# Ranking the experts of a mixture-of-experts layer by token count and giving the three smallest 64 rows

## The chip, the cores and the metric

The kernel runs on one core of a Trainium2 chip. The metric is the device time of one execution in microseconds (us), the median of several runs.

## What is computed

The reference is a model of two parts on 256 tokens with 1024 channels. The first part has two layers (neighbourhood attention, an RWKV recurrence and a convolution side by side, then a feed-forward network), the second part two more layers of another kind. The feed-forward network of the first part's second layer is the mixture of experts (MoE) that the change is about:

```python
logits = (xt @ router).astype(jnp.float32)
top_logit, top_e = lax.top_k(logits, TOP_K)          # 2 of 8 experts per token
gates = jax.nn.softmax(top_logit, axis=-1)
...
def expert_block(args):
    x_blk, e = args
    return _swiglu(x_blk, w_gate[e], w_up[e], w_down[e])   # silu(x Wg) * (x Wu), then Wd
...
y = jnp.zeros_like(xt).at[s_tok].add(yb[dest] * s_gate[:, None].astype(xt.dtype))
```

An expert's weights are `w_gate` and `w_up` of 1024x3584 and `w_down` of 3584x1024, all float32. There are 512 assignments of a token to an expert in all. With the inputs used here the experts 0 to 7 get 66, 72, 53, 98, 54, 53, 64 and 52 of them; this follows from the reference's router and is the same in every run.

## The kernel before

**Arithmetic.** A float32 operand is split in two parts that TensorE (PE) can multiply: hi is the operand rounded, lo is what is left. `split` (L180) makes hi with a cast on ScalarE (ACT, L182) and lo with a subtraction on VectorE (DVE, L183). A product x·w is then three products of parts: x hi by w hi, x lo by w hi, x hi by w lo (`projT`, L267). All of them are issued at L154; transposes on PE at L158.

**Weights.** `wload` (L185) starts a 1 MB load on the SP queue into one of 5 buffers `wr`, and splits the tile in two chunks of 128x1024 into `wh` (ACT) and `wl` (DVE), of which there are 5 buffers each. A `wr` buffer comes free when its second `wl` is written; a `wh` or `wl` buffer when PE has used it.

**One expert.** The MoE runs expert after expert, 0 to 7, each with 128 slots for tokens. First the tokens of a pair of experts are gathered: `one_hot` (L1272, DVE) makes the matrix `oh` of tokens by slots from `pos`, the slot of each token, and 32 products of `oh` with the hi and lo part of the tokens put the gathered tokens, transposed, in PSUM; ACT copies the hi part to `xH` (L1205), DVE the lo part to `xL` (L1206). An expert's 3584 hidden columns are 7 blocks of 512. A block is `gate_up` (L1160): four chunks of `w_gate` and four of `w_up`, 48 products into two PSUM banks, silu on ACT (L1171) and the product of the two, `s`, on DVE (L1172); and `down` (L1175): four transposes of `s`, their split into `aH` (ACT) and `aL` (DVE), and four chunks of `w_down`, 24 products. That is 6 loads, 12 casts, 12 subtractions and 72 products of 512 columns. `down` of a block stands behind `gate_up` of the next. At the expert's end `y` is scaled and split (L1244 on ACT, L1245 on DVE), `back` (L1262) multiplies it with the transposed one-hot matrix `ohT`, and DVE adds the result to `moe_out` (L1251). While expert 7 ends, the second part's first weights are loaded and the residual is added (L1037).

**Routing.** Ahead of the gather DVE compares the logits, makes `sel` (which token has which expert), and PE counts: `pp` holds each token's slot and, in its third row, each expert's count. `pos` (L1130) is the slot, or over 4096 where a token doesn't use the expert. The largest count goes to a register (`most`, L1210); where it is over 128 an extra pass (`overflow`, L1294) runs ahead of expert 2. With these inputs it does not.

**Order.** The instructions of the MoE stand on each engine's queue in an order that a scheduler chose at build time; each engine works through its queue in order.

## Time and profile before

| | us |
|---|---|
| median of 3 runs (2878.35 to 2884.21) | 2883.58 |
| the profiled execution, its own time | 2886.99 |
| its span, first to last instruction | 2885.2 |
| MoE, first gather's first product to the last `w_down` product | 1240.96 to 2283.88 |
| experts 5, 6 and 7, from expert 4's `y` to expert 7's | 1900.28 to 2284.32 |

The span is followed with a profile of one execution: how long each engine (PE with its weight loads PEld, DVE, ACT, POOL and the DMA engines) was busy, which waits ended last (the chain), and single instructions in order of time. Starts are us from the start of the span. "Granted clock" is the share of full speed that TensorE was given in a stretch: 1.00 is 2.4 GHz, 0.5 would be 1.2 GHz.

### The profile page before, as it was taken

To read this page: it belongs to the slowest core of one execution; us is meant where nothing else is said; L and a number is where in the kernel's file an instruction comes from. 1 tells how busy PE (TensorE), PEld (TensorE's weight loads), DVE (VectorE), ACT (ScalarE), POOL (GpSimd) and SP (SyncE) were. 2 spreads that over 40 slices of the span, in tenths; PEclk is the share of its full clock that TensorE was granted. 3 is DMA by queue.
4 is the path that set the end of the run, shared out by engine and by line. 5 is a ranking of instruction groups with operands and counts; after the bars stand their busy time and mean duration, and the time that the engine had idled before them with its cause. 6 is when DMAs were issued, how large, how long until landed. Compare 5 with 4: busy or idle time off the path is not lost. (4 is left out here: it accounts for less than half of the span.)

```text
span 2885.2 us, 42860 instructions
## 1 busy us (share of the span) xinstructions
PE 2750.6 (95%) x17006; PEld 2257.8 (78%) x17006; DVE 1988.4 (69%) x2753; ACT 1468.3 (51%) x2032; POOL 348.5 (12%) x256
## 2 busy tenths in 40 slices
PE   6998999999998879999989999999999999999999
PEld 4677656778886766677867777778777889998999
DVE  4685474322225796488878888888889868856784
ACT  3313243322224332477757777767777646644563
POOL 1420012211001610100000000000000221301120
PEclk9898799999999998999999999999999999999999
DMA  6122155333333224579988999899989835553453
GB/s 227 51 74 74 52 150 193 96 123 94 97 99 105 81 88 140 173 293 352 319 321 325 322 353 344 328 338 362 337 325 349 307 114 175 183 183 117 161 184 109
DMA packets 108098, 585.77 MB, mean 203 GB/s; under 512 B 12657, under 2 KB 19825, under 8 KB 54129
## 3 DMA queue, kind: packets, MB, share of 16 engines
q1 hardware_dynamic: 107888, 582.95, 57.5%
q8 instruction: 136, 2.23, 0.3%
q14 instruction: 74, 0.60, 0.1%
HBM read 580.80 MB, written 2.10 MB: 202 GB/s over the span
## 5 line engine op out<-in xcount | busy, mean ns | idle before, releaser
L183 DVE TENSOR_TENSOR wl<-wr,wh 128x1024 fp32r<-128x1024 f32 x978 | 1169.5, 1225 | 477.9 <-ACT wh L182 465.6
L182 ACT CAST wh<-wr 128x1024 fp32r<-128x1024 f32 x992 | 1003.8, 1044 | 681.1 <-PE psffn L154 193.2
L154 PE MATMUL psmoe<-wh,xH 128*128 128x512 f32 x896 | 354.9, 397 | 3.4 <-ACT wh L182 3.4
L154 PE MATMUL psmoe<-wl,xH 128*128 128x512 f32 x896 | 356.2, 398 | 1.0 <-DVE wl L183 0.7
L154 PE MATMUL psmoe<-wh,xL 128*128 128x512 f32 x896 | 355.5, 397 | 0.0
L154 PEld LDWEIGHTS psmoe<-wl,xH 128*128 128x128 f32 x896 | 168.3, 188 | 45.6 <-DVE wl L183 6.5
L154 PEld LDWEIGHTS psmoe<-wh,xH 128*128 128x128 f32 x896 | 168.4, 188 | 44.4 <-ACT wh L182 5.0
L154 PE MATMUL pssf<-oh,wl 128*128 128x256 f32 x704 | 199.5, 284 | 0.0
L154 PE MATMUL pssf<-ohT,wh 128*128 128x256 f32 x704 | 199.2, 284 | 0.0
L154 PEld LDWEIGHTS psmoe<-wh,xL 128*128 128x128 f32 x896 | 168.4, 188 | 39.1
L154 PE MATMUL pssf<-oh,wh 128*128 128x256 f32 x704 | 198.9, 284 | 0.0
L154 PE MATMUL psmoe<-wh,aL 128*128 128x512 f32 x448 | 178.3, 398 | 2.0 <-DVE aL L183 2.0
L154 PE MATMUL psmoe<-wh,aH 128*128 128x512 f32 x448 | 175.6, 397 | 2.5 <-ACT aH L182 2.5
L154 PE MATMUL psmoe<-wl,aH 128*128 128x512 f32 x448 | 163.3, 400 | 0.0
L1551 POOL TENSOR_SCALAR x<-x,fin 128x256 f32<-128x256 f32 x8 | 12.2, 1542 | 1057.5 <-DMA wr<-w_in 1057.3
L154 PE MATMUL psffn<-h2L,wh 128*128 128x512 f32 x352 | 138.7, 394 | 1.3 <-POOL h2L L257 1.3
L154 PE MATMUL psffn<-h2H,wh 128*128 128x512 f32 x352 | 138.2, 395 | 1.0 <-ACT h2H L256 1.0
L154 PE MATMUL psffn<-h2H,wl 128*128 128x512 f32 x352 | 137.5, 392 | 0.0
L154 PEld LDWEIGHTS pssf<-oh,wl 128*128 128x128 f32 x704 | 135.2, 192 | 0.0
L154 PEld LDWEIGHTS pssf<-ohT,wh 128*128 128x128 f32 x704 | 135.1, 192 | 0.0
L154 PEld LDWEIGHTS pssf<-oh,wh 128*128 128x128 f32 x704 | 135.0, 192 | 0.0
L154 PEld LDWEIGHTS psmoe<-wh,aL 128*128 128x128 f32 x448 | 84.2, 188 | 24.4 <-DVE aL L183 4.4
(476 smaller groups left out, 5624.6 us busy)
## 6 DMA issues: line engine op xcount, KB each, us to landing
wr<-moe_w_gate SPq DMA_DIRECT2D x112, 1024.0 KB, 7.0
wr<-moe_w_up SPq DMA_DIRECT2D x112, 1024.0 KB, 6.6
wr<-moe_w_down SPq DMA_DIRECT2D x112, 1024.0 KB, 7.0
wm<-mod_w SPq DMA_DIRECT2D x96, 512.0 KB, 4.3
wr<-f_up SPq DMA_DIRECT2D x44, 1024.0 KB, 4.9
wr<-w_in SPq DMA_DIRECT2D x52, 512.0 KB, 3.8
wr<-w_in SPq DMA_DIRECT2D x16, 1024.0 KB, 5.0
wr<-f_down SPq DMA_DIRECT2D x16, 1024.0 KB, 5.0
```

Of the source, the lines that this page charges most:

```text
L154: i = self.nc.tensor.matmul(out, lhsT, rhs, start=start, stop=stop, **kw)
L182: self.nc.scalar.copy(H, src)
L183: (eng or self.nc.vector).tensor_sub(L, src, H.bitcast(F32))
L1551: nc.gpsimd.tensor_scalar(x[:, k], x[:, k], fin[:, k:k + 1], None, op0=ALU.mult)
```

## The change

**Ranking.** Between the counting and `pos`, DVE ranks the experts by count, largest first, with ties in order of number; expert 0 gets the key 1024, so it keeps place 0. `pm` is the 8x8 permutation. `pos`, the counts and the gate weights `wt` are permuted into the order of places (`placed`). `who` holds the expert of each place.

**Weights by register.** SP reads seven places of `who` into registers at expert 1; the loads of places 1 to 7 take the address of the weights from the register (`at`).

**Places 5 to 7** have 64 slots. The hi and lo parts of their tokens stand side by side in one stationary operand of 64 + 64 columns, so that one product with w hi and one with w lo give x hi·w in the rows 0 to 63 of PSUM and x lo·w in the rows 64 to 127: a load takes 8 products in place of 12, a block 48 in place of 72. For gate and up the two halves are added ("fold"): ACT copies the rows 64 to 127 to SBUF, DVE adds the rows 0 to 63. Silu works on 64 rows, the product `s` is made on POOL, the transposes are 64 columns wide, and `aH` and `aL` become the halves of one tile. The halves of `w_down`'s result are not folded: `ohT` of these places has the 64 one-hot rows twice, so `back` adds them.

**Gathers.** Places 0 and 1, and 2 and 3, are gathered as before; place 4 alone, 5 and 6 together with 64 products of 64 columns, and 7 alone with 32. `overflow` starts at 64 rows for the small places.

```diff
-                nc.vector.tensor_tensor(pos, pp[:, 0:2], off, ALU.add)
+                cnt = pr.tile([128, 8], F32, name="cnt")
+                key = pr.tile([128, 8], F32, name="key")
+                nc.vector.tensor_copy(cnt, pp[:, 2])
+                nc.vector.tensor_copy(key, cnt)
+                nc.vector.memset(key[:, 0:1], 1024.0)
+                i8 = self.iota[:, 0:8]
+                sq8, lt2 = [128, 8, 8], lt[:, 0]
+                a, c = key[:, None, :].to_broadcast(sq8), key[:, :, None].to_broadcast(sq8)
+                kg, ke = gt[:, 0], eq[:, 0]
+                nc.vector.tensor_tensor(kg, a, c, ALU.is_gt)
+                nc.vector.tensor_tensor(ke, a, c, ALU.is_equal)
+                nc.vector.tensor_tensor(ke, ke, lt2, ALU.mult)
+                nc.vector.tensor_add(kg, kg, ke)
+                rank = pr.tile([128, 8], F32, name="rank")
+                nc.vector.tensor_reduce(rank[:, :, None], kg, AX.X, ALU.add)
+                nc.vector.tensor_tensor(pm, rank[:, None, :].to_broadcast(sq8), i8[:, :, None].to_broadcast(sq8), ALU.is_equal)
+                def placed(o, v):
+                    for tt in range(2):
+                        w = pr.tile(sq8, F32, tag="plw", name=self.nm("plw"), bufs=2)
+                        nc.vector.tensor_tensor(w, pm, v[:, tt, None, :].to_broadcast(sq8), ALU.mult)
+                        nc.vector.tensor_reduce(o[:, tt, :, None], w, AX.X, ALU.add)
+                nc.vector.tensor_tensor(off, pp[:, 0:2], off, ALU.add)
+                placed(pos, off)
...
+                self.at = lambda n, j: A[n][0] if j == 0 else A[n][bass.ds(self.place[j], 1)][0]
...
+                                if e < SMALL:
+                                    self.projT(ps, H, L, xh, xl, [(k, k0 + k) for k in range(2)], slice(0, 128), k0 == 0, k0 == 6)
+                                    continue
+                                for k in range(2):
+                                    self.mm(ps, xh[:, k0 + k], H[:, k], k0 + k == 0, False, chain=ps)
+                                    self.mm(ps, xh[:, k0 + k], L[:, k], False, k0 + k == 7, chain=ps)
...
-                    nc.scalar.activation(s, pp[0], AF.Silu)
-                    nc.vector.tensor_mul(s, s, pp[1])
-                    return s
+                    if e < SMALL:
+                        nc.scalar.activation(s, pp[0], AF.Silu)
+                        nc.vector.tensor_mul(s, s, pp[1])
+                        return s
+                    two = []
+                    for ps in pp:
+                        t = pg.tile([64, 512], F32, tag="fold", name=self.nm("fold"))
+                        nc.scalar.copy(t, ps[64:128])
+                        nc.vector.tensor_add(t, ps[0:64], t)
+                        two.append(t)
+                    nc.scalar.activation(s[0:64], two[0], AF.Silu)
+                    nc.gpsimd.tensor_mul(s[0:64], s[0:64], two[1])
+                    return s[0:64]
...
-                    aL = pg.tile([128, 4, 128], F32R, tag="aL", name=self.nm("aL"))
-                    self.split(aH, aL, pt)
+                    aL = aH[:, :, 64:128] if n == 64 else pg.tile([128, 4, 128], F32R, tag="aL", name=self.nm("aL"))
+                    self.split(aH[:, :, 0:n], aL, pt)
...
+                                if n == 128:
+                                    self.mm(py[o], aL[:, kh * 2 + k], H[:, 0, c], False, False, chain=py[o])
...
+                def gather_small(e0, n, t):
+                    X = pg.tile([128, 8, 2, 128], F32R, tag=t, name=self.nm(t))
+                    for k in range(KT):
+                        ps = self.ps((128, n, 2, 64))
+                        for i, src in enumerate((hmH, hmL)):
+                            for j in range(n):
+                                for tt in range(2):
+                                    self.mm(ps[:, j, i], src[:, tt, k * 128:(k + 1) * 128], oh[:, tt, e0 + j, 0:64], tt == 0, tt == 1, chain=ps)
+                        (nc.vector.tensor_copy if k % 2 else nc.scalar.copy)(X[:, k, 0:n], ps.rearrange("p a b s -> p a (b s)"))
...
+                    if e == 1:
+                        self.place = [None] + [nc.values_load(who[0:1, j:j + 1], engines=(mybir.EngineType.SP,), min_val=0, max_val=7) for j in range(1, E)]
```

**How the order moves.** Line numbers of the changed kernel lie one higher at the helpers (L182 becomes L183, L183 becomes L184) and further on up to a hundred higher. The first place is DVE's queue between the counting and the first one-hot matrix `oh`. Before (`hmL` is the lo part of the tokens, `h` the tokens scaled, `mx` and `over` the largest count):

```order
L1129 TENSOR_SCALAR off<-sel 128x16
L183 TENSOR_TENSOR hmL<-h_9945,hmH 128x512
L1130 TENSOR_TENSOR pos<-psrout_9906,off 128x16
L1146 SCALAR_TENSOR_TENSOR h_9949<-psrout_9930,rr_9875,sb 128x512
L1275 TENSOR_TENSOR oh<-cst,pos 128x2x256
L1149 TENSOR_REDUCE mx<-psrout_9906 128x1
L183 TENSOR_TENSOR hmL<-h_9949,hmH 128x512
L1150 CAST over<-mx 128x1
L183 TENSOR_TENSOR wl_10028<-wr_10021,wh_10027 128x1024
```

In the changed kernel the same stretch, in two pieces; the first begins behind `off` (`cnt`, `key`, `gt`, `eq`, `ixw` and `plw` belong to the ranking):

```order
L1136 COPY cnt<-psrout_9908 128x8
L1159 TENSOR_TENSOR off<-psrout_9908,off 128x16
L1137 COPY key<-cnt 128x8
L184 TENSOR_TENSOR hmL<-h_9965,hmH 128x512
L1138 MEMSET key 128x1
L1176 SCALAR_TENSOR_TENSOR h_9969<-psrout_9950,rr_9877,sb 128x512
L1143 TENSOR_TENSOR gt<-key 128x64
L1144 TENSOR_TENSOR eq<-key 128x64
L1183 COPY ixw<-cnt 128x8
L184 TENSOR_TENSOR wl_10061<-wr_10054,wh_10060 128x1024
L1145 TENSOR_TENSOR eq<-eq,cs_r 128x64
L184 TENSOR_TENSOR hmL<-h_9969,hmH 128x512
```

The second piece follows it and ends with `oh`:

```order
L1146 TENSOR_TENSOR gt<-gt,eq 128x64
L184 TENSOR_TENSOR wl_10079<-wr_10076,wh_10078 128x1024
L1148 TENSOR_REDUCE rank<-gt 128x8
L184 TENSOR_TENSOR wl_10083<-wr_10076,wh_10082 128x1024
L1150 TENSOR_TENSOR pm<-rank,cst 128x64
L184 TENSOR_TENSOR wl_10102<-wr_10099,wh_10101 128x1024
L1156 TENSOR_TENSOR plw_9929<-pm,off 128x64
L1156 TENSOR_TENSOR plw_9932<-pm,off 128x64
L1157 TENSOR_REDUCE pos<-plw_9929 128x8
L1157 TENSOR_REDUCE pos<-plw_9932 128x8
L1156 TENSOR_TENSOR plw_9978<-pm,ixw 128x64
L1368 TENSOR_TENSOR oh<-cst,pos 128x2x256
```

Ahead of `oh` there stand now sixteen small instructions of the ranking and placing in place of one, one `hmL` more, and four subtractions `wl` of the first weight chunks that stood behind it.

The second place is a block of a small expert in its steady state. ACT's queue before, from the silu of a block to the cast of its `aH` (`wh` are the casts of the chunks, a pair for each load):

```order
L1171 ACTIVATE s_19150<-psmoe_19060 128x512
L182 CAST wh_19130<-wr_19128 128x1024
L182 CAST wh_19134<-wr_19128 128x1024
L182 CAST wh_19164<-wr_19162 128x1024
L182 CAST wh_19168<-wr_19162 128x1024
L182 CAST wh_19186<-wr_19184 128x1024
L182 CAST wh_19190<-wr_19184 128x1024
L182 CAST aH_19304<-psmoe_19299 128x512
L182 CAST wh_19209<-wr_19207 128x1024
```

ACT's queue in the changed kernel, from the silu of a block to a cast behind its `aH_19424`:

```order
L1228 ACTIVATE s_19283<-fold_19284 64x512
L183 CAST wh_19302<-wr_19300 128x1024
L183 CAST wh_19306<-wr_19300 128x1024
L1225 COPY fold_19287<-psmoe_19246 64x512
L183 CAST wh_19320<-wr_19318 128x1024
L183 CAST wh_19324<-wr_19318 128x1024
L183 CAST aH_19424<-psmoe_19419 128x4x64
L183 CAST wh_19339<-wr_19337 128x1024
L183 CAST wh_19343<-wr_19337 128x1024
```

Six casts stood between the silu and `aH`; now four stand there and the copy for the fold of `up`, two of them behind that copy, and `aH` stands ahead of the casts of the next gate load (`wr_19337`). DVE's queue before, from the last chunk ahead of `s` to one behind the `aL` made from it:

```order
L183 TENSOR_TENSOR wl_19165<-wr_19162,wh_19164 128x1024
L1172 TENSOR_TENSOR s_19150<-s_19150,psmoe_19105 128x512
L183 TENSOR_TENSOR wl_19169<-wr_19162,wh_19168 128x1024
L183 TENSOR_TENSOR wl_19187<-wr_19184,wh_19186 128x1024
L183 TENSOR_TENSOR wl_19191<-wr_19184,wh_19190 128x1024
L183 TENSOR_TENSOR aL_19305<-psmoe_19299,aH_19304 128x512
L183 TENSOR_TENSOR wl_19210<-wr_19207,wh_19209 128x1024
```

DVE's queue in the changed kernel, over the same piece of a block as ACT's:

```order
L1226 TENSOR_TENSOR fold_19284<-psmoe_19209,fold_19284 64x512
L184 TENSOR_TENSOR wl_19268<-wr_19265,wh_19267 128x1024
L184 TENSOR_TENSOR wl_19272<-wr_19265,wh_19271 128x1024
L184 TENSOR_TENSOR wl_19303<-wr_19300,wh_19302 128x1024
L184 TENSOR_TENSOR wl_19307<-wr_19300,wh_19306 128x1024
L1226 TENSOR_TENSOR fold_19287<-psmoe_19246,fold_19287 64x512
L184 TENSOR_TENSOR wl_19321<-wr_19318,wh_19320 128x1024
L184 TENSOR_TENSOR wl_19325<-wr_19318,wh_19324 128x1024
L184 TENSOR_TENSOR aH_19424<-psmoe_19419,aH_19424 128x4x64
L184 TENSOR_TENSOR wl_19340<-wr_19337,wh_19339 128x1024
```

Two folds have taken the place of `s`, and two `wl`, where three stood, lie between the last of them and the subtraction that fills the second half of `aH`.

## Rows read from the trace of the kernel before

**Rows 1.** Windows, experts 5-7: us, busy PE PEld DVE ACT POOL, clock, DMA, GB/s.

```profile
1900.28:2284.32 384.04, 378.36 (x1689) 301.89 (x1687) 333.72 (x328) 275.10 (x308) 0.00 (x0) 1.00 0.93 344
```

**Rows 2.** Chain that ended last, part of expert 3: start us, us, what.

```profile
1705.34 16.80 PE psmoe L154 x72
1722.14 0.44 PE psmoe L158 x4
```

**Rows 3.** Groups by form, same window: count, busy us, mean ns, idle before.

```profile
L183 DVE TENSOR_TENSOR wl<-wr,wh 128x1024 fp32r<-128x1024 f32 x251 | 293.6, 1219 | 31.5 <-ACT wh L182 29.3 <-PE psmoe L154 0.8
L182 ACT CAST wh<-wr 128x1024 fp32r<-128x1024 f32 x251 | 248.2, 1050 | 18.0 <-PE psmoe L154 17.7
L182 ACT CAST aH<-psmoe 128x512 fp32r<-128x512 f32 x21 | 12.3, 587 | 31.4 <-PE psmoe L158 31.4
L1251 DVE TENSOR_TENSOR moe_out<-moe_out,psmoe 128x512 f32<-128x512 f32 x12 | 7.7, 681 | 0.1
L1245 DVE SCALAR_TENSOR_TENSOR y<-psmoe,gs,y 128x512 fp32r<-128x512 f32 x6 | 4.2, 746 | 6.9 <-ACT y L1244 6.9
L1037 DVE SCALAR_TENSOR_TENSOR x<-moe_out,modt,x 128x256 f32<-128x256 f32 x8 | 3.6, 475 | 0.0
```

**Rows 4.** DVE in time, expert 5: start us, us, instruction [idle before <-releaser].

```profile
1907.19 8.03 DVE L183 TENSOR_TENSOR wl<-wr,wh 128x1024 fp32r<-128x1024 f32 x7
1915.13 0.68 DVE L1172 TENSOR_TENSOR s<-s,psmoe 128x512 f32<-128x512 f32 x1
1915.73 4.62 DVE L183 TENSOR_TENSOR wl<-wr,wh 128x1024 fp32r<-128x1024 f32 x4
```

**Rows 5.** POOL, then DVE, in time, second part of the model.

```profile
2419.65 2.14 POOL L1597 TENSOR_TENSOR moe_out<-moe_out 128x512 f32<-128x512 f32 x1 [13.04 <-DVE moe_out L1639]
...
2449.88 1.30 POOL L1597 TENSOR_TENSOR moe_out<-moe_out 128x512 f32<-128x512 f32 x1 [6.12 <-DVE moe_out L1639]
...
2420.55 1.91 DVE L1638 SCALAR_TENSOR_TENSOR moe_out<-u,prs,moe_out 128x255 f32<-128x255 f32 x2
...
2448.87 0.87 DVE L1639 SCALAR_TENSOR_TENSOR moe_out<-u,prs,moe_out 128x255 f32<-128x255 f32 x2
```

**Rows 6.** Windows in expert 0, columns as in Rows 1.

```profile
1256.00:1266.00 10.00, 10.00 (x45) 8.04 (x44) 9.99 (x11) 9.85 (x11) 0.00 (x0) 1.00 1.01 423
1320.00:1340.00 20.00, 20.00 (x88) 16.08 (x87) 17.80 (x17) 15.31 (x16) 0.00 (x0) 1.00 1.00 380
```

**Rows 7.** DVE, then PE, in time around the first gather.

```profile
1240.13 0.68 DVE L1275 TENSOR_TENSOR oh<-cst,pos 128x512 fp32r<-128x512 f32 x1
1240.73 0.16 DVE L1149 TENSOR_REDUCE mx<-psrout 128x1 f32<-128x8 f32 x1
...
1240.96 0.77 PE L154 MATMUL psmoe<-oh,hmH 128*128 128x256 f32 x2 [1.61 <-DVE mx L1149]
...
1242.37 0.63 PE L154 MATMUL psmoe<-oh,hmL 128*128 128x256 f32 x2
1242.80 0.63 PE L154 MATMUL psmoe<-oh,hmH 128*128 128x256 f32 x2
...
1246.51 0.40 PE L154 MATMUL psmoe<-wh,xH 128*128 128x512 f32 x1
```

**Rows 8.** Instructions of line 1210 by engine: minimum, median, maximum ns.

```profile
L1210 SPq TENSOR_LOAD <-over x1: 469/469/469, 1284.0 to 1284.0; - x1
```

**Rows 9.** PE in order of time at the end of expert 7.

```profile
2283.88 0.63 PE L154 MATMUL psmoe<-wl,aH 128*128 128x512 f32 x2
...
2292.35 0.39 PE L154 MATMUL pssp<-hmH,wh 128*128 128x256 f32 x1 [0.33 <-ACT wh L182]
```

**Rows 10.** Windows where PE waits often, columns as in Rows 1.

```profile
980.00:1000.00 20.00, 14.28 (x58) 11.48 (x60) 17.37 (x24) 4.71 (x7) 16.43 (x9) 0.66 0.16 42
1236.00:1246.00 10.00, 7.32 (x38) 7.28 (x39) 8.10 (x19) 4.62 (x10) 0.00 (x0) 0.56 0.33 111
```

More of the change, by code (lines that the diff above doesn't have):

```diff
@@ L25 @@
 FE = 3584
+SMALL = 5
 FF = 2816
@@ L1167, in gate_up @@
                                 k0 = kh * 4 + i * 2
-                                self.projT(ps, H, L, xh, xl, [(k, k0 + k) for k in range(2)], slice(0, 128), k0 == 0, k0 == 6)
+                                if e < SMALL:
[4 more added lines that the diff above has]
+                                    self.mm(ps, xh[:, k0 + k], L[:, k], False, k0 + k == 7, chain=ps)
@@ L1175, in down @@
+                    nc.scalar.activation(s[0:64], two[0], AF.Silu)
+                    nc.gpsimd.tensor_mul(s[0:64], s[0:64], two[1])
+                    return s[0:64]
                 def down(e, fb, s, py):
[L1176 removed]
+                    n = s.shape[0]
+                    pt = self.ps((128, 4, n))
                     for k in range(4):
[L1178 removed]
+                        self.tp(pt[:, k], s[:, k * 128:(k + 1) * 128], self.ident[0:n, 0:n], chain=pt)
@@ new lines, in moe, with gather @@
+                xs = {}
+                def gather(e0, n, tag):
+                    H, L = [pg.tile([128, 8, 2, 128], F32R, tag=t, name=self.nm(t)) for t in ("xH", "xL")]
+                    for k in range(KT):
+                        ps = self.ps((128, 2, n * 128), tag=tag)
+                        for i, src in enumerate((hmH, hmL)):
+                            for tt in range(2):
+                                self.mm(ps[:, i], src[:, tt, k * 128:(k + 1) * 128], oh[:, tt, e0:e0 + n].rearrange("p a s -> p (a s)"),
+                                        tt == 0, tt == 1, chain=ps)
+                        nc.scalar.copy(H[:, k, 0:n].rearrange("p a s -> p (a s)"), ps[:, 0])
+                        nc.vector.tensor_copy(L[:, k, 0:n].rearrange("p a s -> p (a s)"), ps[:, 1])
+                    for i in range(n):
+                        xs[e0 + i] = H[:, :, i], L[:, :, i]
@@ new lines, in gather_small @@
+                def gather_small(e0, n, t):
+                    X = pg.tile([128, 8, 2, 128], F32R, tag=t, name=self.nm(t))
+                    for k in range(KT):
+                        ps = self.ps((128, n, 2, 64))
+                        for i, src in enumerate((hmH, hmL)):
+                            for j in range(n):
+                                for tt in range(2):
+                                    self.mm(ps[:, j, i], src[:, tt, k * 128:(k + 1) * 128], oh[:, tt, e0 + j, 0:64], tt == 0, tt == 1, chain=ps)
+                        (nc.vector.tensor_copy if k % 2 else nc.scalar.copy)(X[:, k, 0:n], ps.rearrange("p a b s -> p a (b s)"))
+                    for i in range(n):
+                        xs[e0 + i] = X[:, :, i], None
@@ new lines, in moe @@
+                for e in range(E):
+                    if e == 0:
+                        gather(0, 2, "pp")
+                    elif e == 2:
+                        self.overflow(out, hmH, hmL, oh, ohT, gs, pos, wt, most, pg)
+                        self.one_hot(oh, pos, 2, 0)
+                        gather(2, 2, "ax")
+                    elif e == 4:
+                        self.one_hot(oh, pos, 4, 0, 1)
+                        for j in range(SMALL, E):
+                            self.one_hot_small(oh, pos, j)
+                        gather(4, 1, "ax")
+                    elif e == 5:
+                        gather_small(5, 2, "xH")
+                    elif e == 7:
+                        gather_small(7, 1, "xL")
+                    xh, xl = xs[e]
@@ L1228, in moe @@
                         nc.vector.reciprocal(mx, mx)
-                        nc.vector.tensor_tensor(wt, wt, mx.to_broadcast([128, 2, 8]), ALU.mult)
+                        nc.vector.tensor_tensor(lg, wt, mx.to_broadcast([128, 2, 8]), ALU.mult)
+                        for tt in range(2):
+                            w = pg.tile([128, 8, 8], F32, tag="s", name=self.nm("wtw"))
+                            nc.vector.tensor_tensor(w, pm, lg[:, tt, None, :].to_broadcast([128, 8, 8]), ALU.mult)
+                            nc.vector.tensor_reduce(wt[:, tt, :, None], w, AX.X, ALU.add)
                     if e % 2 == 0:
@@ L1298, in overflow @@
             w_ = lambda i: pg.tile([128, 8, 2, 128], F32R, tag=("xH", "xL")[i], name=self.nm("wo")).bitcast(F32).rearrange("p a b c -> p (a b c)")
+            for e in range(E):
+                self.one_hot(oh, pos, e, 128 if e < SMALL else 64, 1)
             for e in range(0, E, 2):
-                self.one_hot(oh, pos, e, 128)
                 self.slots(oh, ohT, gs, wt, e)
```

53 lines of the change are left out of this document (24 added, 29 removed).

## The prediction

> **What bounds the kernel now.** I looked first at the stretch in which the small experts will stand, experts 5 to 7 [rows 1]. The reader is to see that PE is busy for 378.36 of 384.04 us at a granted clock of 1.00, the higher of its two levels, 2.4 GHz, while DVE has 333.72, ACT 275.10, POOL nothing, and the DMA engines a share of 0.93. The chain of waits says the same: a block is 16.80 us of 72 products and 0.44 us of transposes, 17.24 us, with nothing between [rows 2]. A product is thus 16.80 / 72 = 0.233 us. So products taken away shorten the stretch, but only down to what comes next, and DVE and the DMA engines are close behind.
>
> **The change part by part.** *The block of a small expert.* PE: 48 × 0.233 + 0.44 = 11.6 us at most, 5.6 less than now. The loads stay at six of 1.0486 MB, 6.29 MB. In two windows the DMA engines were busy throughout, at 423 and at 380 GB/s [rows 6]; a block then takes 14.9 or 16.55 us. I take the lower rate, the one of the longer window. DVE: seven subtractions in a row take 8.03 us [rows 4], 1.147 each, so twelve are 13.76. An operation of 128x512 that reads PSUM keeps DVE for 0.60 (from 1915.13 to 1915.73 [rows 4]). A fold has the same 512 elements in each row, 0.61 with its start; two are 1.22. The lo half of `aH` has half of them: 0.35, an estimate from that 0.60. The product `s` goes from DVE to POOL. Together 15.33 us.
>
> Two things are added on DVE's side. POOL's product has no row of its own in this shape; the nearest is POOL's product of the same row length, 1.30 us by itself and 2.14 beside DVE [rows 5]. In that second case two DVE operations that otherwise take 0.87 took 1.91 [rows 5]: 1.04 us lost on DVE each time. The bounds are 0 (nothing overlaps) and 1.3 (DVE stands for the whole of POOL's operation); I take the measured 1.04. The second is the way from the fold of `up` to `aL`: POOL up to 2.14, four transposes 0.44, the cast of `aH` on ACT (0.59 for twice the size [rows 3]), and only then ACT's next cast `wh`, 1.05 [rows 3], for which DVE waits. From the end of the fold that is 2.14 + 0.44 + about 0.4 + 1.05 = 4.0 us, with the hand-overs some 4.35. DVE has meanwhile two subtractions, the stop and the lo half: 2.3 + 1.04 + 0.35 = 3.7. So it waits about 0.7, between 0 (POOL undisturbed at 1.30) and 1.5. Before, six casts stood there and hid it all.
>
> Sum of a block on DVE: 15.33 + 1.04 + 0.7 = 17.07 us against 17.24 on PE: almost nothing is gained. Without the two additions the DMA engines set 16.55; with both at their upper ends it is 15.33 + 1.3 + 1.5 = 18.1. ACT has twelve casts at some 0.97, two copies, a silu and `aH`, under 14 us, and is no bound.
>
> *The three experts.* 21 blocks are 21 × 17.07 = 358.5 us. To them come what DVE does at the experts' ends: 4.2 + 7.7 for `y` and `moe_out`, 3.6 for the residual [rows 3], and about 2.4 for its half of the gathers' copies, 17.9 in all. And DVE's waits while PE gathers. At the higher clock a product of 256 columns takes half of the 0.233 us, 0.12; narrower ones have no row here, and I give them the same price as their upper end, so 64 and 32 products are 7.7 and 3.8 us. At the three ends together that is 0 (DVE has five free `wl` buffers, 5.7 us, to work ahead) to 11.5; I take 6.8. Sum 358.5 + 17.9 + 6.8 = 383.2 against 384.04: **−0.8 us**.
>
> *The routing.* Here PE stands and waits for DVE: the first gather product starts at 1240.96, just when `oh` is written [rows 7], and the first product of expert 0 follows the gather at once, at 1246.51 [rows 7], so a late `oh` is paid in full. In the new order 15 more small instructions stand ahead of `oh`, an `hmL`, and four `wl`. A small one takes 0.16 [rows 7], with its start 0.17: 2.55. `hmL`, 128x512, is 0.60 as above. Four `wl` at 1.147 are 4.59. **+7.7 us**. The `wl` are not lost work, but behind `oh` they cost nothing, since PE was busy without a pause there [rows 6]. The bounds: 3.2 if the subtractions fall into waits of DVE, 9 if each small one waits for the one before it.
>
> *The registers.* Eight reads in place of one on SP, 0.469 us each [rows 8], and one more register instruction before each of 294 loads. Loads stand far enough ahead, five `wr` buffers and as many `wh` and `wl`; if that cover is gone at expert 1, the seven reads cost at most 7 × 0.47 = 3.3 us. I take 0.
>
> *The end.* From the last MoE product at 2283.88 to the second part's first weights at 2292.35 [rows 9] PE waits for little. With DVE full, fewer of those chunks are split ahead: **+1**, between 0 and 4.6 (four chunks). The gather that moves from experts 6 and 7 to smaller ones, the permuted `wt` (a few 0.17 us instructions) and the other experts' blocks, which remain at 17.24, cost nothing more, since PE sets their time.
>
> Sum: −0.8 + 7.7 + 1 = +7.9 us on the profiled execution's 2886.99. That one is 0.12% above the median of the runs shown; on the median, 2883.58 + 7.9 = **2891.5 us**.
>
> A rule of the Trainium skill speaks against the change. The rows show the core loading at 380 to 423 GB/s [rows 6]. "DMA: Bandwidth & Descriptors", section "Where 436 GB/s comes from", says that transfers from HBM to SBUF are held to about 358 GB/s for each core. By it a block's loads would take 17.57 us, the three experts about 10 us more than in my sum, and the whole about 2902. The trace goes above that figure, so the sum doesn't use it; slower loads have a place among the rivals.
>
> **The rivals.**
> *The loads or DVE's bare work are the bound (0.30).* POOL's product falls where DVE waits anyway, and ACT runs ahead far enough. For it: in this stretch DVE waited 31.5 us for casts [rows 3], time in which a stop costs nothing. Against it: with DVE the last to be ready there is less such time. A block is then between 15.6 (DVE's 15.33 and a little, loads at 423 GB/s) and the loads' 16.55. The whole is 7.9 − 21 × (17.07 − block): at 16.55 it is −3, 2880.6; at 15.6 it is −23, 2860.6; in the middle, at 16.2, −10.4, **2873**. It decides from a block below 16.4 us on: there the whole is 5.8 us faster.
>
> *The way through the fold is longer (0.14).* Behind the copy for the fold of `up` ACT's casts wait until PE has done the last product of `up`, which waits for DVE's last `wl` of it; two engines then hold each other up in turn. Against it: two `wl` stand on DVE between that chunk and the fold. At 18.1 us for a block the stage is 21 × 1.03 = 22 us longer than in my sum: 2913.
>
> *The loads are slower than in expert 0 (0.04).* If they never go above this stage's mean of 344 GB/s [rows 1], a block takes 18.3 us: 21 × 1.2 = 26 more than in my sum, 2917. Against it stand both windows [rows 6].
>
> *TensorE's clock falls (0.09).* With 11.6 of 17 us of work PE has pauses in each block. In one stretch with 14.28 of 20 us busy the granted clock was 0.66, in one with 7.32 of 10, behind a longer wait, 0.56 [rows 10], so part of it at the lower level of 1.2 GHz. There two products of 256 columns, as many columns as one of 512, started 0.43 us after the two before [rows 7]. A block is then 48 × 0.43 + 0.44 = 21.1, 4.0 over DVE's; in a quarter of the blocks that is 21 us, 2913. Against it: the pauses are about a microsecond each, spread over the block. "TensorE: Matmul & The Clock Gate", section "HAM oscillation — how this bites in real kernels", of the Trainium skill describes a kernel whose products are shorter than the wait for their next operand, so that it falls to the lower clock at each step.
>
> That the change doesn't do what it says: with 53, 53 and 52 tokens the three small places hold all of theirs, and place 1 has 98, so the extra pass stays out; the order shows 48 products a block. I give it nothing.
>
> **How the numbers follow.** A measurement of this kernel can tell about 0.2%, 5.8 us, from no change. The forecast has 0.43. Its own range is 2882 to 2903: the routing's 3.2 to 9, the register reads' 3.3, the end's 4.6 and part of the block's spread. I put 0.24 of it over 2889.3 (slower), 0.18 within and 0.01 under. The first rival gives 0.26 faster and 0.04 same (at 16.4 to 16.55), the three others 0.27 slower. Together 0.27 faster, 0.22 same, 0.51 slower. The range goes from 2864, a block of 15.8 us in the first rival, to 2914; outside lie the slower loads, half of the clock and of the longer fold, and the far end of the first rival.
>
> **What would show it.** In the profile after, a small expert's block should have DVE busy or stopped throughout, about 17.1 us long, with PE waiting for `wl` and `wh` over five microseconds a block; `oh` written near 1248.5 and the first gather there; experts 0 to 4 unchanged between their `y`; POOL's `s` at about 2 us, with a DVE operation beside it some 1 us too long. I am wrong if blocks take under 16.7 or over 17.7 us, if DVE's operations beside POOL aren't longer, or if the gather starts before 1244.

## The result and the profile after

The changed kernel takes 2918.93 us in the median of 4 runs (2914.35 to 2924.86); the kernel before takes 2882.01 (2878.35 to 2884.21, 4 runs). The ratio is 1.0131, 95% interval 1.0108 to 1.0153, so 31 to 44 us slower. I had forecast 2891.5 with a range of 2864 to 2914: slower, as forecast, but by four to five times as much, and outside the range.

The profiled execution took 2920.04 us, its span is 2918.3 against 2885.2 before. Experts 5 to 7 now run from 1889.15 to 2319.45, 430.3 us against 384.04 [rows 1]. The windows of that stretch, of ten microseconds in expert 5's gather and of one block in its steady state (columns as in rows 1):

```profile
1889.15:2319.45 430.30, 340.95 (x1248) 243.19 (x1248) 339.74 (x348) 287.38 (x349) 79.43 (x21) 0.85 0.83 306
1900.00:1910.00 10.00, 10.00 (x45) 9.71 (x45) 1.27 (x3) 1.12 (x3) 0.00 (x0) 0.50 0.01 2
2011.99:2030.14 18.15, 14.84 (x54) 9.68 (x53) 15.33 (x16) 13.43 (x17) 3.31 (x1) 0.91 0.93 367
```

PE and the loads both have less to do in a microsecond than before (PE busy for 340.95 of 430.30 us, DMA share 0.83, where it was 378.36 of 384.04 and 0.93 [rows 1]), and DVE is no busier: nothing is full. The granted clock is 0.85 over the stretch, and 0.50, the lower level of 1.2 GHz, in the gather. The groups of instructions from 2060 to 2160 say who waits (busy us, mean ns, idle before and its releaser):

```profile
L184 DVE TENSOR_TENSOR wl<-wr,wh 128x1024 fp32r<-128x1024 f32 x63 | 73.3, 1217 | 5.4 <-ACT wh L183 5.2
...
L1229 POOL TENSOR_TENSOR s<-s,fold 64x512 f32<-64x512 f32 x6 | 19.8, 3308 | 94.8 <-DVE fold L1226 94.8
...
L159 PE MATMUL psmoe<-cst,s 64*128 64x64 f32 x24 | 3.3, 271 | 16.7 <-POOL s L1229 16.7
L184 DVE TENSOR_TENSOR aH<-psmoe,aH 128x256 fp32r<-128x256 f32 x6 | 2.5, 425 | 13.0 <-ACT aH L183 13.0
...
L183 ACT CAST aH<-psmoe 128x256 fp32r<-128x256 f32 x6 | 2.2, 372 | 20.8 <-PE psmoe L159 20.8
```

POOL's `s` takes 3308 ns, where before a product of the same row length took 1.30 us by itself [rows 5]. PE's transposes wait for it (16.7 us for six blocks), ACT's cast `aH` for them, and DVE's lo half of `aH` for that cast, 13.0 us for six blocks. In order of time, two blocks of POOL:

```profile
1936.68 5.51 POOL L1229 TENSOR_TENSOR s<-s,fold 64x512 f32<-64x512 f32 x1 [10.40 <-DVE fold L1226]
...
2011.99 3.31 POOL L1229 TENSOR_TENSOR s<-s,fold 64x512 f32<-64x512 f32 x1 [14.62 <-DVE fold L1226]
```

and DVE around them:

```profile
1935.85 0.68 DVE L1226 TENSOR_TENSOR fold<-psmoe,fold 64x512 f32<-64x512 f32 x1 [1.09 <-ACT fold L1225]
1936.46 4.61 DVE L184 TENSOR_TENSOR wl<-wr,wh 128x1024 fp32r<-128x1024 f32 x4
```

```profile
2011.23 0.68 DVE L1226 TENSOR_TENSOR fold<-psmoe,fold 64x512 f32<-64x512 f32 x1
2011.84 2.34 DVE L184 TENSOR_TENSOR wl<-wr,wh 128x1024 fp32r<-128x1024 f32 x2
2016.48 0.42 DVE L184 TENSOR_TENSOR aH<-psmoe,aH 128x256 fp32r<-128x256 f32 x1 [2.30 <-ACT aH L183]
2017.42 6.90 DVE L184 TENSOR_TENSOR wl<-wr,wh 128x1024 fp32r<-128x1024 f32 x6 [0.52 <-ACT wh L183]
```

The reader is to see when POOL ends. Beside two subtractions that end at 2011.84 + 2.34 = 2014.18 its product lasts until 2015.30; beside four that end at 1941.07 it lasts until 1942.19. Both times that is about 1.1 us after DVE's last subtraction: what is left of POOL's product once DVE stands still is nearly the whole of it. In all 21 blocks it ends 1.12 us after the last of two to five such subtractions, and none of them is lengthened. ACT in the second of the two blocks:

```profile
2010.15 0.58 ACT L1225 COPY fold<-psmoe 64x512 f32<-64x512 f32 x1 [0.28 <-PE psmoe L155]
...
2016.08 0.37 ACT L183 CAST aH<-psmoe 128x256 fp32r<-128x256 f32 x1 [3.44 <-PE psmoe L159]
```

Its copy for the fold of `up` waits only 0.28 us for PE; the long wait, 3.44 us, is the one at `aH`, behind POOL's `s` and the transposes.

The other engine to look at is PE while it has all 72 products. The chain in expert 3, which the change leaves as it was:

```profile
1710.08 16.52 PE psmoe L155 x72
1726.61 0.44 PE psmoe L159 x4
```

A block of 72 products takes 16.52 us; before it was 16.80 [rows 2]. And around the first gather, the first cast of the tokens' hi part on ACT, `oh` on DVE and the first gather product on PE:

```profile
1223.98 0.62 ACT L183 CAST hmH<-h 128x512 fp32r<-128x512 f32 x1 [2.58 <-DVE h L1176]
```

```profile
1238.19 0.68 DVE L1368 TENSOR_TENSOR oh<-cst,pos 128x512 fp32r<-128x512 f32 x1
```

```profile
1239.02 0.76 PE L155 MATMUL psmoe<-oh,hmH 128*128 128x256 f32 x2 [9.10 <-DVE ix L1157]
```

The same cast before:

```profile
1233.40 0.62 ACT L182 CAST hmH<-h 128x512 fp32r<-128x512 f32 x1 [2.58 <-DVE h L1146]
```

From that cast to the first gather product it was 1240.96 − 1233.40 = 7.6 us [rows 7], and is 1239.02 − 1223.98 = 15.0. The cast itself came 9.4 us earlier; the instructions up to it are the same in both kernels but for one small copy on DVE (`ixw`), and in the profiles of the experiments it stands between 1217.7 and 1239.5, so that is the spread of executions.

The spans differ by 33.1 us, and that is made up of: −9.4 up to that cast; +7.5 to the first gather; −9.2 from there to expert 4's `y` (659.3 before, 650.1 after); +46.3 in experts 5 to 7; −2.0 behind them.

### The profile page after: what moved, and what is told of

Same layout as the page of the kernel before. It is cut to its first block, busy times and chain, and to the rows that moved or that the text cites. A ratio compares the mean times of both kernels' runs of the same rounds, so it can differ in the third digit from the quotient of the medians.

```text
span 2918.3 us, 42695 instructions
## 1 busy us (share of the span) xinstructions
PE 2696.3 (92%) x16566; PEld 2193.1 (75%) x16566; DVE 2002.1 (69%) x2802; ACT 1475.8 (51%) x2072; POOL 418.7 (14%) x277
## 4 chain that ended last, share of the span: by engine, by line
PE 37%; DVE 5%; POOL 3%; issue 3%; ACT 2%; ACTq 0%; DVEq 0%; POOLq 0%
PE psmoe L155 16%; PE pssf L155 13%; PE pssp L155 4%; DVE wl L184 3%; POOL s L1229 3%; PE psssg L155 2%; ACT wh L183 1%; PE pssat L155 1%; PE psmoe L159 1%; DVE fold L1226 1%; PE pssat L159 0%; DVE moe_out L1344 0%; ACT s L1228 0%; ACT y L1337 0%; DVE x L1038 0%
## 5 line engine op out<-in xcount | busy, mean ns | idle before, releaser
L184 DVE TENSOR_TENSOR wl<-wr,wh 128x1024 fp32r<-128x1024 f32 x978 | 1181.6, 1239 | 459.2 <-ACT wh L183 446.6
L183 ACT CAST wh<-wr 128x1024 fp32r<-128x1024 f32 x992 | 1000.5, 1044 | 645.3 <-PE psffn L155 193.2
L155 PE MATMUL psmoe<-wl,xH 128*128 128x512 f32 x784 | 321.5, 411 | 10.0 <-DVE wl L184 9.9
L155 PE MATMUL psmoe<-wh,xH 128*128 128x512 f32 x784 | 315.6, 404 | 3.6 <-ACT wh L183 3.6
L155 PE MATMUL psmoe<-wh,xL 128*128 128x512 f32 x672 | 269.4, 401 | 0.0
L1229 POOL TENSOR_TENSOR s<-s,fold 64x512 f32<-64x512 f32 x21 | 79.4, 3782 | 1010.6 <-DVE fold L1226 1010.6
L155 PEld LDWEIGHTS psmoe<-wl,xH 128*128 128x128 f32 x784 | 151.9, 194 | 65.5 <-DVE wl L184 33.1
L155 PEld LDWEIGHTS psmoe<-wh,xH 128*128 128x128 f32 x784 | 153.0, 195 | 36.8 <-ACT wh L183 6.5
L155 PEld LDWEIGHTS psmoe<-wh,xL 128*128 128x128 f32 x672 | 129.5, 193 | 27.4 <-ACT wh L183 0.2
L155 PE MATMUL psmoe<-wh,aL 128*128 128x512 f32 x280 | 110.4, 394 | 0.6 <-DVE aL L184 0.6
L155 PEld LDWEIGHTS psmoe<-wl,aH 128*128 128x128 f32 x448 | 86.7, 206 | 28.7 <-DVE wl L184 11.3
```

Source lines behind the costliest of these rows:

```text
L155: i = self.nc.tensor.matmul(out, lhsT, rhs, start=start, stop=stop, **kw)
L183: self.nc.scalar.copy(H, src)
L184: (eng or self.nc.vector).tensor_sub(L, src, H.bitcast(F32))
L1229: nc.gpsimd.tensor_mul(s[0:64], s[0:64], two[1])
```

## The experiments

Three questions came from this. What makes experts 5 to 7 longer: POOL's product that can't go on (called the port theory: POOL and DVE both read SBUF then, and one would keep the other out), or TensorE's clock? What do ranking and registers cost by themselves? And why do the unchanged products take 16.52 us? Times of before in each comparison are those of the same chip in the same hours, so kernels of different experiments are best compared by their ratios.

### 1. `s` on DVE

```diff
-                    nc.gpsimd.tensor_mul(s[0:64], s[0:64], two[1])
+                    nc.vector.tensor_mul(s[0:64], s[0:64], two[1])
```

> The changed kernel with one word altered: the product s of the small experts is made on DVE, not on POOL. Port theory: in the changed kernel POOL's product lasts 3.31 to 6.66 us because it doesn't go on while DVE works through its subtractions, and the chain fold, s, transposes, aH, next cast waits for it. On DVE it takes about 0.6 us, a block becomes 15.3 + 0.6 = 15.9 us of DVE or what the loads allow (16.6 to 17.1), the three experts take some 375 us in place of 430, and the whole about 2864. Clock theory: the granted clock of 0.85 in that stretch is what lengthens it; then it stays near 430 and the whole over 2905.

Measured: 2869.19 us in the median (10 runs), before 2879.82 (25), ratio 0.997 (0.995 to 0.999). One word turns 1.3% slower into 0.3% faster. Experts 5 to 7 take 368.7 us. The stretch and one block (columns as in rows 1), then DVE in that block:

```profile
1893.18:2261.86 368.68, 326.32 (x1248) 209.06 (x1248) 348.13 (x369) 288.24 (x349) 0.00 (x0) 0.96 0.92 355
2066.88:2082.76 15.88, 14.02 (x54) 8.43 (x53) 15.84 (x17) 13.57 (x17) 0.00 (x0) 1.00 1.01 410
```

```profile
2066.88 0.68 DVE L1229 TENSOR_TENSOR s<-s,fold 64x512 f32<-64x512 f32 x1
2067.49 2.34 DVE L184 TENSOR_TENSOR wl<-wr,wh 128x1024 fp32r<-128x1024 f32 x2
2069.76 0.41 DVE L184 TENSOR_TENSOR aH<-psmoe,aH 128x256 fp32r<-128x256 f32 x1
2070.10 6.88 DVE L184 TENSOR_TENSOR wl<-wr,wh 128x1024 fp32r<-128x1024 f32 x6
```

DVE is busy for 15.84 of 15.88 us, with no wait at `aH` or behind it, and the loads run at 410 GB/s. The wait is gone with POOL's product, as the port theory has it; the clock theory falls, as the clock came back to 1.00 by itself when the wait was gone. The runs show that POOL's product stands still beside DVE; that a port of SBUF is the reason is argued, not shown.

### 2. A wait more: DVE stands still for POOL

```diff
                     nc.gpsimd.tensor_mul(s[0:64], s[0:64], two[1])
+                    t = pg.tile([64, 8], F32, tag="mark", name=self.nm("mark"))
+                    self.mark = nc.vector.tensor_copy(t, s[0:64, 0:8]).ins.name
...
+        if self.after_mark is not None:
+            self.tc.add_manual_dep(i.ins, self.after_mark, NOSYNC, reason="behind the mark")
```

> The changed kernel with s still on POOL, and one tiny DVE copy that reads s, put ahead of the two subtractions that stand between the fold of up and aH, so that DVE stands still while POOL makes s. It only adds a wait and an instruction. Port theory: POOL's product takes about 1.2 us, DVE loses 1.3 us a block but the 2.8 us that it waited for aH and the next cast go; a block is near 16.9 us, the whole about 2874. Rival (DVE is the bound and every wait adds): 21 times 1.3 us more, about 2945.

Measured: 2888.92 us (9 runs), ratio 1.0032 (1.001 to 1.0055): 30 us less than the changed kernel by an instruction and a wait that were added. POOL, then DVE, in one block:

```profile
1993.06 1.26 POOL L1232 TENSOR_TENSOR s<-s,fold 64x512 f32<-64x512 f32 x1 [15.53 <-DVE fold L1229]
```

```profile
1992.23 0.68 DVE L1229 TENSOR_TENSOR fold<-psmoe,fold 64x512 f32<-64x512 f32 x1
1994.36 0.16 DVE L1234 COPY mark<-s 64x8 f32<-64x8 f32 x1 [1.44 <-POOL s L1232]
1994.46 2.36 DVE L185 TENSOR_TENSOR wl<-wr,wh 128x1024 fp32r<-128x1024 f32 x2
1996.74 0.42 DVE L185 TENSOR_TENSOR aH<-psmoe,aH 128x256 fp32r<-128x256 f32 x1
1997.08 6.89 DVE L185 TENSOR_TENSOR wl<-wr,wh 128x1024 fp32r<-128x1024 f32 x6
```

POOL's product now takes 1.26 us. DVE waits 1.44 us for it, and no longer 2.30 + 0.52 behind `aH`; a block is 1994.36 to 2011.14, 16.8 us, where 16.9 was expected (columns as in rows 1):

```profile
1994.36:2011.14 16.78, 14.05 (x52) 8.43 (x52) 15.34 (x16) 13.43 (x16) 1.27 (x1) 1.00 0.97 377
```

The granted clock is 1.00 here with `s` still on POOL, against 0.91 in the changed kernel's block, so the clock follows the wait. In six of the 21 blocks one subtraction had begun ahead of POOL's product, which then took 2.1 us. The whole was expected at 2874 and came out 15 us over it; the profiled execution itself took 2876.98, and where the rest lies was not found.

### 3. Subtractions of half the length

```diff
+            for c in (slice(0, 512), slice(512, 1024)):
+                self.nc.vector.tensor_sub(v(L)[:, c], v(src)[:, c], v(H.bitcast(F32))[:, c])
```

> The changed kernel with each subtraction wl of the small experts cut in two of half the length, in the same order. If POOL goes on only when DVE stands still, s stays at 3.3 us and more, DVE has about 0.6 us a block more to do, the whole is about 2932. If POOL waits only for the end of the operation that DVE is in, s falls to 2 us or less, and the whole to about 2905.

Measured: 2964.65 us (4 runs), ratio 1.0293 (1.0259 to 1.0326), more than either theory gave. POOL and DVE in one block:

```profile
1988.24 5.25 POOL L1235 TENSOR_TENSOR s<-s,fold 64x512 f32<-64x512 f32 x1 [15.81 <-DVE fold L1232]
```

```profile
1987.47 0.68 DVE L1232 TENSOR_TENSOR fold<-psmoe,fold 64x512 f32<-64x512 f32 x1 [0.66 <-ACT fold L1231]
1988.08 4.29 DVE L188 TENSOR_TENSOR wl<-wr,wh 128x512 fp32r<-128x512 f32 x7
```

The scheduler put seven halves behind the fold, not four. POOL's product lasts 5.25 us and ends 1.1 us after the seventh half (1988.08 + 4.29 = 1992.37, and 1993.49). Six times an operation of DVE ended and the next began without a pause, and POOL got next to nothing done at any of them. So here POOL doesn't wait for the end of one operation, it waits for a pause. That holds in 16 of the 21 blocks. In the other five, all at the beginning of an expert, POOL's product takes 1.58 to 1.65 us, for example:

```profile
1915.66 1.59 POOL L1235 TENSOR_TENSOR s<-s,fold 64x512 f32<-64x512 f32 x1 [695.77 <-ACT wh L184]
```

```profile
1915.45 8.37 DVE L188 TENSOR_TENSOR wl<-wr,wh 128x512 fp32r<-128x512 f32 x12
```

There POOL got in after the first half, and DVE lost by it: its twelve halves took 8.37 us, where twelve others, from 1996.96 on, take 7.32. So the end of an operation can be enough. What decides between the two was not found.

### 4. Ranking and registers, without small experts

```diff
-SMALL = 5
+SMALL = 8
```

with the gathers in pairs, as before.

> Ranking, permutation and loads by register as in the changed kernel, but all places with 128 rows, gathered in pairs, so no small expert. Theory: the later first gather costs 7.5 us and the seven register reads nothing, so 7 to 9 us over the kernel before, and experts 5 to 7 take 384 us. Rival: the register reads and the register instruction before each load hold the loads up; then 15 us or more over before, with PE waiting for casts in experts 1 to 7.

Measured: 2861.53 us (10 runs), ratio 0.9944 (0.992 to 0.9967): not 8 us slower than before, but 18 faster. In its profile the first gather stands 15.05 us behind the first `hmH` cast, so the 7.5 us are there; the seven register reads cost nothing that shows. But a block of 72 products takes 16.52 us in this kernel too. Something in the change speeds up products that it doesn't touch, and against this kernel the small experts cost 54 us (ratios 1.0131 and 0.9944), not 37; in the profiles experts 5 to 7 take 430.3 us against 378.5 here.

### 5. The kernel before again, and with 288 unused bytes

What all kernels with 16.52 have in common are two tiles, `who` and `pm`, in a pool ahead of the MoE's operands. I first took the same kernel before for its profile, then added only the two tiles, which nothing uses:

```diff
             over = pe.tile([128, 1], I32, name="over")
+            who = pe.tile([128, 8], I32, name="who")
+            pm = pe.tile([128, 8, 8], F32, name="pm")
```

> The kernel before, once more, for its profile beside the next kernels. Its 72 products took 16.80 us a block in the first profile, 16.52 in all five profiles of kernels with the ranking. If that was the chip or the execution, it is 16.5 here; if it is the kernel, 16.8, and the wait ahead of expert 2's gather is about 9.6 us again, against 5.6.

> The kernel before with the two tiles of the ranking, who and pm, put at their place in the pool and used by nothing: no instruction more, but the tiles behind them lie 288 bytes further in each partition. If the place in SBUF sets the spacing of the products, a block takes 16.5 us and the whole is about 18 to 22 us under before; if not, 16.8 and the same time as before.

Measured: the kernel before took 2882.15 us in its run. With the two tiles 2856.93 (4 runs), before 2883.98 (8), ratio 0.9906 (0.9869 to 0.9943): 27 us for nothing but a place in memory. The two profiles differ by 23.1 us: 13.8 of them lie between the first `hmH` cast and expert 7's `y` (1051.3 and 1037.5 us), 5.1 behind that, and 4.1 ahead of the cast, in the spread of executions. Blocks in the chain of the one and of the other:

```profile
1717.66 16.80 PE psmoe L154 x72
```

```profile
1707.91 16.52 PE psmoe L154 x72
```

### 6. Which shift: 32 and 64 bytes, and the changed kernel put back

In the kernel before, the tiles that PE reads in the MoE (`xH`, `xL`, `aH`, `aL`, `y`) and `s` begin 32 bytes past a multiple of 64 bytes; `xH` at 67168. With 288 bytes more they begin at a multiple of 64. The next three kernels put in 32 or 64 bytes in place of 288, and 32 more in the changed kernel:

```diff
+            pad = pe.tile([128, 8], I32, name="pad")
```

(and 16 columns for 64 bytes).

> The kernel before with one unused tile of 32 bytes in the pool ahead of the MoE's tiles: xH, xL, aH, aL and s then begin at a multiple of 64 bytes (xH at 67200, before at 67168), as they did with 288 bytes. If that is what sets the spacing of the products, 16.5 us for 72 products and some 20 to 27 us under before; if it takes the shift by 288, 16.8 and no gain.

> The same with 64 bytes: the tiles begin 32 bytes past a multiple of 64 again (xH at 67232). If the 64-byte boundary decides, 16.8 us for 72 products and the time of before; if any shift helps, 16.5.

> The changed kernel with 32 bytes more, which takes its tiles off the multiple of 64: blocks of 72 products take 16.8 us again, and the whole is 15 to 25 us over the changed kernel's 2919, about 2940. That is then what the change costs without the shift that its two new tiles brought with them. If the boundary matters only in the kernel before, it stays at 2919.

Measured: with 32 bytes 2862.9 us (10 runs), before 2883.68 (21), ratio 0.9932 (0.9901 to 0.9963); with 64 bytes 2872.49 (9 runs), 0.9964 (0.9935 to 0.9993); the changed kernel with 32 bytes more 2936.74 (4 runs), 1.0175 (1.0117 to 1.0233). A block in the chain of each, in that order:

```profile
1709.08 16.52 PE psmoe L154 x72
```

```profile
1728.94 16.80 PE psmoe L154 x72
```

```profile
1731.84 16.80 PE psmoe L155 x72
```

16.52 at a multiple of 64, 16.80 off it, three times out of three. (With 32 and with 288 bytes `xH` begins at 67200 and 67456, which are multiples of 128 too, so 64 and 128 are not told apart.) With 64 bytes the whole is still some 10 us under before, which was not expected; its experts 1 to 7 take 910.9 us from `y` to `y`, as before (911.7). In its profile the difference lies ahead of the first `hmH` cast, in the spread of executions, and behind expert 7's `y` (595.9 us, 600.9 before); its cause was not found. So a part of what the unused bytes save is not that of the 72 products. Without the shift that `who` and `pm` bring with them the change costs 1.75%, some 50 us. In the profiles the shift is worth 9.2 us to the changed kernel, all of it between the first gather and expert 4's `y` (650.1 us with it, 659.3 without); experts 5 to 7, where PE has time to spare, take 430.3 and 429.7.

### 7. Small experts without ranking

Experts 5 to 7 by their numbers, with fixed addresses, no ranking, `s` on DVE (the two tiles stay). With other inputs an expert that has more than 64 tokens would have the rest done in the extra pass.

> Small experts without the ranking: experts 5, 6 and 7 (53, 64 and 52 tokens here) have 64 rows, weights by fixed address, s on DVE; the two tiles of the ranking stay in the pool. Against the run with ranking and s on DVE (2869) the first gather is 7.5 us earlier, all else alike: about 2861. If the loads by register cost something too, it is under 2857.

Measured: 2860.08 us (5 runs), ratio 0.9911 (0.988 to 0.9943). The time is what was expected, in part by luck: in the profile, expert 0's `y` stands 137.3 us behind the first `hmH` cast against 145.0 with the ranking in experiment 1, so the 7.5 us are gained, but some 5 are given back between expert 1's `y` and expert 2's, 143.8 us against 139.1. The first product of expert 2's gather, here and then in experiment 1, with PE's idle time before it in brackets:

```profile
1503.10 0.77 PE L155 MATMUL psmoe<-oh,hmH 128*128 128x256 f32 x2 [8.96 <-DVE oh L1332]
```

```profile
1504.02 0.76 PE L155 MATMUL psmoe<-oh,hmH 128*128 128x256 f32 x2 [5.80 <-DVE oh L1368]
```

PE stands 8.96 us in place of 5.80, for an `oh` that comes later, behind a branch that all engines take there.

### 8. TensorE given its 72 products back

```diff
+                                    self.mm(ps, zero, H[:, k], False, False, chain=ps)
```

> The changed kernel with s on DVE and a third product in each chunk of the small experts, of a stationary of zeros, which adds nothing: TensorE has its 72 products again, the rest stays. If the saved products are worth what the trace says, a block goes from 15.9 us to 16.5 + 0.4 = 17.0 and the three experts from 369 to about 390; if the falling clock and the waits of TensorE eat the saving, it stays under 376. The granted clock in that stretch should be 1.00 but for the gather.

Measured: 2923.31 us (3 runs), ratio 1.0154 (1.0098 to 1.0209), and 439.9 us for experts 5 to 7, not 390:

```profile
1881.23:2321.09 439.86, 407.96 (x1750) 326.41 (x1751) 361.05 (x369) 303.51 (x349) 0.00 (x0) 0.94 0.83 303
```

The expectation missed, for the clock as well (0.94): a block takes 18.55 us in experts 5 and 7 and some 20.4 in expert 6. The scheduler put another order (on DVE the lo half of `aH` now stands ahead of `s`), and behind its transposes PE waits for a cast and for a subtraction, about 0.5 us each in a block of expert 5. So this run changes more than the number of products and doesn't price them by themselves. Why the three experts take 50 us more than expected is open.

### 9. A version against both

No ranking, experts 4 to 7 small, all four gathered at once by 32 products of 256 columns, `s` on DVE, tiles at a multiple of 64:

```diff
+                                self.mm(ps[:, :, i], src[:, tt, k * 128:(k + 1) * 128], oh[:, tt, 4:8, 0:64], tt == 0, tt == 1, chain=ps)
+                        nc.scalar.copy(X[0][:, k], ps[:, 0:2].rearrange("p a b s -> p a (b s)"))
+                        nc.vector.tensor_copy(X[1][:, k], ps[:, 2:4].rearrange("p a b s -> p a (b s)"))
```

> A version meant to beat both: no ranking, the four experts 4 to 7 with 64 rows (54, 53, 64 and 52 tokens; more go to the extra pass), gathered at once with 32 products of 256 columns, s on DVE, tiles on the multiple of 64. Against the run with three small experts (2860): expert 4 gains some 7 us, the gathers of 64 and 32 narrow products go (some 11 and 7 us with the clock that fell there). About 2840, and blocks of the small experts of 15.9 to 16.5 us. If the loads are the bound by then, at 385 GB/s, it stays over 2850.

Measured: 2819.49 us (5 runs), before 2883.68, ratio 0.9791 (0.974 to 0.9843): 64 us off the 2883.68, and about 100 under the changed kernel. Experts 4 to 7 take 120.1, 115.5, 116.1 and 118.6 us. Most of experts 5 to 7 (columns as in rows 1):

```profile
1880.00:2220.00 340.00, 296.20 (x1117) 179.55 (x1117) 337.70 (x352) 278.29 (x333) 0.00 (x0) 1.00 0.98 380
```

The whole is 20 us better than expected. As ranking, gather and the number of small experts changed together, the run doesn't price any of them alone. DVE is busy 337.70 of 340 us and the loads fill 0.98 of the DMA engines' time: two engines' limits reached at once, at a clock of 1.00.

## Why the prediction was wrong

**The step that failed: what POOL and DVE do to each other.** I read from rows 5 that DVE loses 1.04 us when POOL works beside it, and let POOL take 2.14 at most. In the blocks of the small experts it is the other way round. DVE lost nothing (2.34 us for two subtractions, as in experiment 1 without POOL), and POOL took 3.31 us in the steady state, up to 6.66 where DVE had more to do. The wait that I had put at 0.7 us (between 0 and 1.5) was 2.30 for `aH` and 0.52 for the next cast. My sum of DVE's own work was right: 15.33 expected, and 15.33 busy in the block above, and 15.33 + 2.30 + 0.52 = 18.15 us is just that block's length. So of the 17.07 that I forecast, the mechanism of the second addition was right and its size was off by 2.1 us, and the first addition was nothing: +1.1 us a block, 23 us in 21 blocks. That it is POOL's wait is shown by experiment 1 (wait gone, 15.88), experiment 2 (POOL 1.26 as soon as DVE stands) and experiment 3 (5.25 with seven halves in a row).

What I overlooked in rows 5 stands just ahead of them on DVE:

```profile
2419.42 1.22 DVE L183 TENSOR_TENSOR wl<-wr,wh 128x1024 fp32r<-128x1024 f32 x1
```

This one subtraction ends at 2420.64, and POOL's product at 2421.79, 1.15 us later. So the 2.14 us were a wait for one subtraction and then the product, and DVE's next operation lost the time. I used them as POOL's price beside any number of subtractions.

Two of my three signs of being wrong came true by this: blocks over 17.7 us, and operations of DVE that are no longer beside POOL. The third, a gather before 1244, came true only because the whole execution stood 9.4 us earlier. The rival of a longer way through the fold put a block at 18.1 us, which is the measured length, but by luck: it had ACT wait for PE at the fold's copy, and that wait is 0.28 us.

The Trainium skill, "SBUF — State Buffer", section "🔬 SBUF: two separate sides", says that DVE with two SBUF inputs and GpSimd share a port pair as an exclusive lock, that whichever starts first has it for the whole instruction and that the other fully blocks. The runs agree that POOL blocks, and rows 5 and five blocks of experiment 3 go as the rule says; that POOL blocks over a run of two to eight instructions of DVE, to the end of the last, as in every block of the changed kernel (two to five there), is more than "the whole instruction" says. By the rule I would have expected POOL's product to take about 1.15 + 1.3 = 2.4 us, an estimate.

**The ends of the experts.** For 17.9 + 6.8 us that I had besides the 21 blocks, the trace has 430.3 − 21 × 18.15 = 49. With `s` on DVE (experiment 1) the same sum is 368.7 − 21 × 15.88 = 35, so of the 24 us over my sum some 14 go with POOL's `s`, which took up to 6.66 us in the first blocks of experts 5 and 7, and some 10 stay. Part of these is the gather of places 5 and 6. I gave its 64 products of 64 columns 0.12 us each as an upper end. On PE, in order of time, its first and last four:

```profile
1894.71 1.06 PE L155 MATMUL psmoe<-oh,hmH 128*128 128x64 f32 x4 [0.19 <-DVE moe_out L1344]
...
1907.53 1.04 PE L155 MATMUL psmoe<-oh,hmL 128*128 128x64 f32 x4
```

Four take 0.855 us, 0.214 each, at the granted clock of 0.50 of the window above: 13.7 us and not 7.7, and the same in experiment 1. The price itself was right for the higher clock. In expert 7's gather, while the clock was still 1.00, two products start 0.22 us after the two before:

```profile
2183.87 0.39 PE L155 MATMUL psmoe<-oh,hmL 128*128 128x64 f32 x2
2184.09 0.39 PE L155 MATMUL psmoe<-oh,hmH 128*128 128x64 f32 x2
```

The wide gather of experiment 9 has no stretch at the lower clock. What made the clock fall in the narrow one, and where the other 4 us lie, was not separated.

**The clock as a rival** had 0.09 and came about, but as a companion: 0.85 over the stretch, and 0.96, and 1.00 in a block, as soon as `s` was on DVE, with the same 48 products a block.

**The routing**, +7.7 expected, 7.5 measured from cast to gather; right, and right in its parts (`oh` behind the four subtractions). **The registers**, 0 expected: nothing seen; the seven reads took 0.26 to 0.47 us, 0.27 in the median, where the one before took 0.469 [rows 8]. **The end**, +1 expected: −2.0.

**A term that was missing.** I wrote that the blocks of the other experts remain at 17.24 us. They became 16.96, as two new tiles moved PE's operands to a multiple of 64 bytes. In the kernel before that is worth 0.28 us in each block of 72 products and 13.8 us of the MoE; 20 to 27 us of the whole came with it (experiments 5 and 6), a part of them not by the products. In the changed kernel it hid part of the loss: without it the loss is some 50 us, with it 37. The profile of the changed kernel without the shift differs from before by +7.5 us up to the first gather, nothing from there to expert 4's `y` (659.3 in both), +45.7 in experts 5 to 7 and −1.3 behind, 51.9 in all; the shift takes 9.2 off the second of these.

**The loads.** I took 380 GB/s and 16.55 us a block as the limit of the first rival; in experiment 1 a block took 15.88 us at 410 GB/s. The first rival, with `s` somewhere else than on POOL, was the right picture of what the change could be. The figure of 358 GB/s that the Trainium skill gives in "DMA: Bandwidth & Descriptors", section "Where 436 GB/s comes from", was passed in this kernel by every window shown here that the loads filled: 380 and 423 GB/s [rows 6], 410 in experiment 1, 380 over 340 us in experiment 9.

## What to carry to other kernels

An operation moved from a full DVE to an idle POOL is not off the critical path if what comes next waits for it: look for a row in which POOL works beside a dense run of the very DVE operations, and read who waits for whom, not only how much is lost. Before a gain or loss is put down to an edit, compare a stretch that the edit doesn't touch (here 72 products in an earlier expert); if that has moved as well, look at where the tiles lie. A wait added at the right place can be worth more than the work it delays: DVE standing still for 1.4 us a block saved 30 us.

## What the runs showed of the hardware that was not expected

- POOL's 64x512 product takes 1.26 us when DVE stands still (experiment 2). In all blocks of the changed kernel and 16 of 21 of experiment 3 it ends 1.1 us after the last of two to eight subtractions that DVE does back to back, and DVE's own times don't change (2.34 us for two with POOL beside them and without). In five blocks of experiment 3 it got in between two subtractions, and DVE lost 1.0 us.
- 72 products of 512 columns take 16.80 us when the stationary operands begin 32 bytes past a multiple of 64 in SBUF and 16.52 when they begin at one: 0.2333 and 0.2294 us each, in 13 profiles without exception (4 and 9). Which of the shifted tiles it is, and whether 64 or 128 bytes is the measure, was not tried.
- Ahead of expert 2 all engines take a branch. PE stood 8.96 us there without the ranking and 5.80 and 5.55 with it (in this order experiment 7, experiment 1 and the changed kernel); with only the two tiles it was 9.12. Why the ranking saves these 3 us was not found.
